# Keeping the low part of K in both partition halves, and stacking high and low compressed probabilities on 128 partitions

## The chip, the cores and the metric

The kernel runs on one core of a Trainium2 chip. A core has a matmul engine (TensorE, PE in the rows; its loads of the stationary operand are listed apart as PEld), two engines for elementwise work (VectorE or DVE, ScalarE or ACT), a slower general one (GpSimd or POOL) and an engine that issues transfers (SyncE or SP). They run their own instruction streams and meet at semaphores. The metric is the device time of one execution in microseconds, lower is better.

## The reference, cut to what matters

The program is a stack of transformer pieces on 512 tokens of width 1024, in 32-bit floats: a gated feed-forward block, a mixer with two kinds of attention, attention to a memory of 256 tokens, a second feed-forward block, sliding-window attention, and a pooling layer. The change touches the scores of three attentions with heads of 64 channels, and one small product:

```python
# forgetting attention ("fox"), 8 heads, causal
sc = einsum('bhqd,bkhd->bhqk', q, k) + c_q - c_k;  p = masked_softmax(sc);  o = p @ v
# "nsa", 8 heads in 2 groups: compressed keys, selected blocks, window
s_c = einsum('bsgjd,bcgd->bgjsc', qg, kc) + bias_c;  p_c = masked_softmax(s_c)
o_c = einsum('bgjsc,bcgd->bsgjd', p_c, vc)
o_s = softmax(qg @ k_s + bias) @ v_s          # all 8 blocks are selected: causal over 512
o_w = softmax(qg @ k_w + bias) @ v_w          # window of 512: causal over 512
o = g0 * o_c + g1 * o_s + g2 * o_w
# sliding-window attention with sinks ("swa"), 16 heads, 4 of K and V, window 128
s = q @ k / 8;  p = softmax over 2 blocks of 128 and the sink;  o = p @ v
```

## The kernel before, in words

Every matmul is made precise by splitting. A 32-bit value x is kept as a high part h (x rounded by a copy to the matmul's own 32-bit format, on ScalarE) and a low part x − h (a subtraction, on VectorE); lines 77 to 91 have the helpers `copy`, `low` and `split`. A projection of the width 1024 is eight steps of three matmuls each (lines 116 to 118: high·high, high·low, low·high) of 128 rows by 512 columns, with weights that arrive by a transfer of 512 KB and are split on arrival.

An attention with heads of 64 channels handles two heads per tile of 128 partitions. `stacked` (line 92) makes for each of the two heads e a tile q whose one half of the partitions holds the high part and the other half the low part of the same head. `doubled` (line 98) makes for K a tile per head with the high part in both halves, so that one matmul over 128 rows yields q_high·k_high + q_low·k_high. The low part of K is one tile `kl` for both heads, head e in half e. The second matmul of a score, lines 403 and 1159, uses only these 64 rows of `q` and of `kl`, and adds q_high·k_low in the same bank.

A `causal_unit` (fox and nsa, line 387) is one head: four score steps with 128, 256, 384 and 512 columns, each of two matmuls (lines 402 and 403; in fox a third one, line 405, adds the causal mask), followed on VectorE by the bias and the maximum (line 407), on ScalarE by the exponential (line 411), on VectorE by the reciprocal of the sum (line 415), and on GpSimd by the scaling of the probabilities (line 420). Four "turns" transpose the probabilities on TensorE (line 430) and split them, four "products" multiply by V (lines 442 and 443). An `swa_unit` (line 1139) has two score steps of four matmuls each (line 1158 and line 1159 alternate), the scaling on line 1179, two turns (line 1193) and two products (line 1209).

`run` (line 173) writes TensorE's order: a slot is one score step, a turn that was due some slots later, a product one or two slots after its turn, and between them projection steps from a backlog, spread evenly. TensorE keeps to that order; the other engines' order is laid out by a scheduler. In nsa each head also starts from the compressed product: lines 884 and 885 multiply the same `vcb` (high and low of compressed V, on 64 partitions) by the high and then the low compressed probabilities (`pch`, `pcl`, 64 partitions each). Fox has 4 pairs of heads, one unit a head; nsa 4 pairs, with two units a head; swa 8 pairs.

Of the kernel before, what the change touches and what calls it, by code (L numbers as in the profile page):

```python
# [38 lines left out]
def tile_net(ctx: ExitStack, tc: tile.TileContext, A: dict, out: bass.AP):  # L39
# [9 lines left out]
    def nm(s):  # L49
        uid[0] += 1  # L50
        return f"{s}_{uid[0]}"
# [46 lines left out]
    def doubled(pair, lo, t):  # L98
        for e in range(2):
            rows, other = slice(64 * e, 64 * e + 64), slice(64 - 64 * e, 128 - 64 * e)  # L100
            copy(pair[e][rows, :], t[rows, :])
            copy(pair[e][other, :], t[rows, :])
            low(lo[rows, :], t[rows, :], pair[e][rows, :])

# [281 lines left out]

    def causal_unit(pp, qk, e, bias, diag, coef, v, first, last, open_acc, close_acc, needs=()):
        rows = slice(64 * e, 64 * e + 64)
        st = {}

        def score(i):
            def go():
                if i == 0:
                    st["p"] = pp.tile([P, 1280], F32, tag="P", bufs=2, name=nm("P"))
                    st["nmx"] = small(4, "nmx")
                    st["sm"] = small(4, "sm")
                q, kd, kl = qk()
                pr, nmx, sm = st["p"], st["nmx"], st["sm"]
                n = P * (i + 1)
                b = scb()  # L400
                c = slice(P * i, P * (i + 1))
                nc.tensor.matmul(b[:, :n], q[:, c], kd[:, :n], start=True, stop=False)  # L402
                nc.tensor.matmul(b[:, :n], q[rows, c], kl[rows, :n], start=False, stop=not diag)  # L403
                if diag:
                    nc.tensor.matmul(b[:, P * i : n], ident_bf, cmask_bf, start=False, stop=True)
                sc = pp.tile([P, S], F32, tag="S", bufs=2, name=nm("S"))
                nc.vector.tensor_tensor_reduce(
                    out=sc[:, :n], in0=b[:, :n], in1=bias(i), op0=OP.add, op1=OP.min,
                    scale=-1.0, scalar=3e38, accum_out=nmx[:, i : i + 1])
                w = pr[:, OFF[i] : OFF[i] + n]  # L410
                nc.scalar.activation(w, sc[:, :n], AF.Exp, scale=-1.0,
                                     bias=nmx[:, i : i + 1], accum_out=sm[:, i : i + 1])
                if i % 2:
                    g = slice(i - 1, i + 1)
                    nc.vector.reciprocal(sm[:, g], sm[:, g])
                    if coef is not None:
                        nc.vector.tensor_mul(sm[:, g], sm[:, g], coef[:, g])
                    for z in (i - 1, i):
                        w = pr[:, OFF[z] : OFF[z] + P * (z + 1)]
                        nc.gpsimd.tensor_scalar(w, w, sm[:, z : z + 1], 1.0, op0=OP.mult,  # L420
                                                op1=OP.mult)
            return go
# [100 lines left out]
    def compress_steps(mp, sb, which, kch, kcl, vcb, tails):  # L523
# [28 lines left out]
        def tail():  # L552
# [10 lines left out]
            else:  # L563
# [3 lines left out]
                for g in range(2):  # L567
                    rw = slice(32 * g, 32 * g + 32)
                    split(vcb[rw, g, 0, :], vcb[rw, g, 1, :], b2[rw, :64])

        hw = mp.tile([P, S], F32, tag=("on0", "yf5")[which], name=nm("hw"))
# [3 lines left out]
    def mixer(acc, rep, next_tile, aside):  # L575
        with area("mix") as mp:
# [10 lines left out]
            nc.vector.memset(kcl.bitcast(F32), 0.0)  # L587
            vcb = mp.tile([64, 2, 2, HD], F32R, name="vcb")
            nc.vector.memset(vcb.bitcast(F32), 0.0)
# [46 lines left out]
            with area("fox") as fp:  # L636
# [51 lines left out]
                with area("foxq") as xp, area("att") as ap:  # L688
                    units = []
                    for p in range(4):  # L690
                        qk = {}

                        def fox_steps(p, z, qk):
                            names = ("d0", "d1", "kl") if z else ("q0", "q1")
                            for a in names:
# [9 lines left out]
                            if z:  # L705
                                return project_steps(4 + p, None, doubled, pair, qk["kl"])
                            return project_steps(p, 0.125, stacked, pair)
# [24 lines left out]
            with area("nsa") as np_, area("att") as ap:  # L732
                on += [mp.tile([P, S], F32, tag=f"on{k}", name=nm("on")) for k in range(4)]
                yf += [mp.tile([P, S], F32, tag=f"yf{k}", name=nm("yf")) for k in range(5, KD)]
                vsw = np_.tile([P, NQ, 4, 2, HD], F32R, name="vsw")
                ks = [[np_.tile([P, S], F32R, name=nm("ks")) for _ in range(3)]
                      for _ in range(2)]
# [10 lines left out]
                for p in range(4):  # L748
# [8 lines left out]
                    if p == 0:  # L757
                        each(query_steps(0, st))
                        for br in range(2):
                            each(project_steps(10 + br, None, doubled, ks[br][:2], ks[br][2]))  # L760
                        each(token_major_steps(A["mvsw"], rcol, NQ, xh, xl, store_v(vsw, (0, 4))))
                        needs = ()
                    else:
                        while log.left() < 36 * p - 20:
                            log.add(*side.pop(0))
                        needs = (log.add(query_steps(p, st), KD),)
# [28 lines left out]
    def fox_units(p, xp, ap, qk, vf, ofh, ofl, needs):  # L795
        res = {}
        units = []
        for e in range(2):
            h = 2 * p + e

            def close(acc_b, e=e):
# [6 lines left out]
            units.append(causal_unit(  # L808
                ap, lambda e=e: (qk[f"q{e}"], qk[f"d{e}"], qk["kl"]), e,
                lambda i, e=e: qk["cb", e][:, : P * (i + 1)], True, None,  # L810
# [20 lines left out]
    def nsa_units(np_, ap, p, st, ks, vsw, kch, kcl, vcb, gates, valid, o, needs):  # L831
# [34 lines left out]
        def turn():  # L866
            pc = st["pc"]
            bt = trb()
            for i in range(NQ):
                nc.tensor.transpose(bt[0:64, P * i : P * (i + 1)],  # L870
                                    pc[:, 2 * i : 2 * i + 2, :].rearrange("p e c -> p (e c)"),
                                    ident)
            pch = np_.tile([64, S], F32R, tag="pch", bufs=1, name=nm("pch"))
            pcl = np_.tile([64, S], F32R, tag="pcl", bufs=1, name=nm("pcl"))
            split(pch, pcl, bt[0:64, :])
            st["ph"] = pch, pcl

        units = [Unit([score(0), score(1)], [turn], [None], needs, 2)]
        for e in range(2):
            h = 4 * e + p  # L880

            def lead(acc_b, e=e):
                vc = pair_cols(vcb[:, e])
                nc.tensor.matmul(acc_b, vc, st["ph"][0], start=True, stop=False)
                nc.tensor.matmul(acc_b, vc, st["ph"][1], start=False, stop=False)

            acc = Accumulator(lead)
            for br in range(2):
                units.append(causal_unit(
                    ap, lambda br=br, e=e: (st["q"][e], ks[br][e], ks[br][2]), e,  # L890
                    lambda i, e=e: st["tb"][e][:, 384 - P * i :], False,
# [144 lines left out]
    def attn2(acc1, accg, next_tile):  # L1036
        with area("swa") as mp:
# [27 lines left out]
            for t2 in range(2):  # L1065
                kt = [mp.tile([P, S], F32R, name=nm("kt")) for _ in range(3)]
                t = tmp()
                nc.vector.tensor_mul(t, bk[t2], r)
                doubled(kt[:2], kt[2], t)
                ks.append(kt)  # L1070
# [31 lines left out]
            for m in range(KD):  # L1102
# [11 lines left out]
                for e in range(2):  # L1114
# [3 lines left out]
                    def close(acc_b, e=e, m=m, st=st):  # L1118
# [3 lines left out]
                        if e == 1:  # L1122
                            st["o"] = st["t"]
                            combine(m, st)

                    units.append(swa_unit(mp, st, ks[t2][e], ks[t2][2], e, band, nsk[:, hq : hq + 1],
                                          lambda j, kv=kv: pair_cols(vt[:, j, kv]), close,
# [11 lines left out]
    def swa_unit(mp, qs, kd, kl, e, band, nsk, v, close, needs):  # L1139
        rows = slice(64 * e, 64 * e + 64)  # L1140
        st = {}

        def score(i2):
            def go():
# [7 lines left out]
                for z in range(2):  # L1152
# [5 lines left out]
                    nc.tensor.matmul(b[:, d], q[:, c], kd[:, ks], start=True, stop=False)  # L1158
                    nc.tensor.matmul(b[:, d], q[rows, c], kl[rows, ks], start=False, stop=True)  # L1159
                for z in range(2):  # L1160
# [373 lines left out]
```

## Time and profile before

| what | value |
|---|---|
| median of 3 runs | 1761.22 us (1760.43 to 1761.32) |
| span of the profiled execution, first to last instruction | 1759.5 us |
| TensorE busy | 1737.4 us, 99% of the span, 8308 matmuls |
| weight loads (PEld) | 1396.9 us, 79% |
| VectorE, ScalarE, GpSimd | 966.9 us (55%), 753.6 us (43%), 231.7 us (13%) |
| DMA | 184.19 MB, mean 105 GB/s |

The span is that of one profiled execution; the median is taken from runs of their own, 1.7 us longer. TensorE's busy time counts matmuls that overlap in its pipeline, so the start of one lies before the end of the one ahead, and a mean duration is not the rate at which matmuls follow one another. That rate is read from the chain of waits, whose pieces run from one matmul's end to the next one's end, or from the starts in the timeline. Bracketed figures in a timeline row are the idle time before the instruction and what ended it.

### The profile page before, as it was taken

What the parts mean: (1) busy time and instruction counts of PE and PEld (TensorE: products, weight loads), DVE (VectorE), ACT (ScalarE), POOL (GpSimd) and SP (SyncE); (2) the same over time, 40 slices, a digit from 0 to 9 for tenths busy, and PEclk for the clock granted to TensorE, in tenths of its full rate; (3) what the DMA queues carried; (4) which work ended last, traced back from release to release, by engine and by line L of the source; (5) the groups of instructions that cost most, each with busy time, mean ns of one, the idle gap of its engine ahead of it and who ended that gap; (6) DMA issues with size and microseconds to landing.
All of it is one profiled execution on the core that took longest, in us unless ns stands there. A gap on an engine that the chain in (4) does not pass through costs nothing.

```text
span 1759.5 us, 22066 instructions
## 1 busy us (share of the span) xinstructions
PE 1737.4 (99%) x8308; PEld 1396.9 (79%) x8308; DVE 966.9 (55%) x1718; ACT 753.6 (43%) x1350; POOL 231.7 (13%) x315
## 2 busy tenths in 40 slices
PE   8999999999999999999999999999999999999997
PEld 6888878888778777777988888888888877788887
DVE  7333433336685566667655444433333677876674
ACT  6222222235675555545444432222233566644242
POOL 2000000003221222203001200000011034421001
PEclk9999999999999999999999999999999999999999
DMA  5222244433243122036531522222344321133232
GB/s 191 96 96 96 95 142 118 127 115 108 79 144 106 37 67 78 29 93 205 172 108 48 192 96 89 92 96 96 93 134 123 110 70 51 49 132 124 92 121 78
DMA packets 66255, 184.19 MB, mean 105 GB/s; under 512 B 7979, under 2 KB 13883, under 8 KB 66148
## 3 DMA queue, kind: packets, MB, share of 16 engines
q1 hardware_dynamic: 59300, 171.25, 30.0%
q10 hardware_dynamic: 6848, 11.54, 1.8%
q8 instruction: 65, 1.06, 0.2%
q14 instruction: 42, 0.34, 0.1%
HBM read 170.14 MB, written 15.24 MB: 105 GB/s over the span
## 4 chain that ended last, share of the span: by engine, by line
PE 96%; DVE 2%; ACT 1%; DMA 1%; issue 0%; SPq 0%; POOL 0%; DVEq 0%; ACTq 0%
PE mm L116 21%; PE mm L117 20%; PE mm L118 20%; PE tr L118 6%; PE tr L116 6%; PE tr L117 6%; PE tr L430 2%; PE sc L403 2%; PE pv L320 1%; PE pv L321 1%; PE pv L322 1%; PE sc L1159 1%; PE tr L1193 1%; PE pv L443 1%; PE pv L442 1%; PE sc L402 1%
## 5 line engine op out<-in xcount | busy, mean ns | idle before, releaser
L78 ACT ACTIVATE wh<-wr 128x1024 fp32r<-128x1024 f32 (+2 forms) x292 | 294.7, 1010 | 672.8 <-PE mm L117 348.3
L81 DVE TENSOR_TENSOR wl<-wr,wh 128x1024 fp32r<-128x1024 f32 (+2 forms) x291 | 342.0, 1176 | 174.6 <-ACT wh L78 170.4
L116 PE MATMUL mm<-xh,wh 128*128 128x512 f32 x872 | 359.2, 412 | 5.9 <-ACT wh L78 5.8
L117 PE MATMUL mm<-xl,wh 128*128 128x512 f32 x872 | 347.4, 398 | 0.2
L118 PE MATMUL mm<-xh,wl 128*128 128x512 f32 x872 | 346.6, 397 | 0.0
L222 POOL TENSOR_TENSOR acc<-acc,t 128x512 f32<-128x512 f32 (+1 forms) x55 | 74.8, 1367 | 959.0 <-ACT t L221 958.8
L116 PEld LDWEIGHTS mm<-xh,wh 128*128 128x128 f32 x872 | 165.9, 190 | 39.2 <-ACT wh L78 6.4
L118 PEld LDWEIGHTS mm<-xh,wl 128*128 128x128 f32 x872 | 164.9, 189 | 39.6 <-DVE wl L81 0.2
L117 PEld LDWEIGHTS mm<-xl,wh 128*128 128x128 f32 x872 | 165.5, 190 | 32.9 <-DVE xl L89 2.7
L118 PE MATMUL tr<-xh,wl 128*128 128x512 f32 x424 | 168.2, 397 | 0.5 <-DVE wl L81 0.5
L116 PE MATMUL tr<-xh,wh 128*128 128x512 f32 x424 | 168.1, 396 | 0.0
L117 PE MATMUL tr<-xl,wh 128*128 128x512 f32 x424 | 168.1, 396 | 0.0
L116 PE MATMUL mm<-hh,wh 128*128 128x512 f32 x352 | 138.9, 395 | 0.0
L117 PE MATMUL mm<-hl,wh 128*128 128x512 f32 x352 | 138.9, 395 | 0.0
L118 PE MATMUL mm<-hh,wl 128*128 128x512 f32 x352 | 138.9, 395 | 0.0
L355 DVE TENSOR_TENSOR t<-t,tr 128x512 f32<-128x512 f32 x44 | 30.3, 688 | 143.9 <-PE tr L118 142.5
L78 ACT ACTIVATE ph<-tr 128x512 fp32r<-128x512 f32 (+3 forms) x136 | 63.8, 470 | 102.6 <-PE tr L430 72.6
L118 PEld LDWEIGHTS tr<-xh,wl 128*128 128x128 f32 x424 | 79.9, 188 | 20.4 <-DVE wl L81 0.9
L117 PEld LDWEIGHTS tr<-xl,wh 128*128 128x128 f32 x424 | 79.9, 188 | 19.5
L116 PEld LDWEIGHTS tr<-xh,wh 128*128 128x128 f32 x424 | 79.8, 188 | 19.3
L81 DVE TENSOR_TENSOR pl<-tr,ph 128x512 fp32r<-128x512 f32 (+3 forms) x136 | 72.1, 531 | 37.0 <-ACT ph L78 35.5
L352 DVE TENSOR_TENSOR t<-mm,rstd 128x512 f32<-128x512 f32 x44 | 30.4, 691 | 112.1 <-PE mm L118 112.1
(344 smaller groups left out, 2994.4 us busy)
## 6 DMA issues: line engine op xcount, KB each, us to landing
wr<-in_f2gu_dram SPq DMA_DIRECT2D x44, 512.0 KB, 3.2
wr<-in_f1gu_dram SPq DMA_DIRECT2D x42, 512.0 KB, 3.2
wr<-in_mfm_dram SPq DMA_DIRECT2D x32, 512.0 KB, 3.2
xd<-xs ACTq DMA_DIRECT2D x40, 256.0 KB, 2.0
wr<-in_ain_dram SPq DMA_DIRECT2D x18, 512.0 KB, 3.3
wr<-in_f1d_dram SPq DMA_DIRECT2D x16, 512.0 KB, 3.6
xs<-xd SPq DMA_DIRECT2D x32, 256.0 KB, 3.3
wr<-in_f2d_dram SPq DMA_DIRECT2D x16, 512.0 KB, 3.6
```

The source lines that it names most:

```text
L78: nc.scalar.activation(o, i, AF.Copy, scale=scale)
L81: (eng or nc.vector).tensor_sub(o, i, h.bitcast(F32))
L116: nc.tensor.matmul(o, sh, mh, start=start, stop=False)
L117: nc.tensor.matmul(o, sh, ml, start=False, stop=False)
L118: nc.tensor.matmul(o, sl, mh, start=False, stop=stop)
L222: (nc.vector if last else nc.gpsimd).tensor_add(acc, acc, q[:, :n])
L320: mm(b, sh[k][:, tk], hi[:, c], start=first, stop=False, skip_group_check=True)
L321: mm(b, sh[k][:, tk], lo[:, c], start=False, stop=False, skip_group_check=True)
L352: nc.vector.tensor_mul(a, pg, r)
L355: nc.vector.tensor_mul(h, a, pu)
L403: nc.tensor.matmul(b[:, :n], q[rows, c], kl[rows, :n], start=False, stop=not diag)
L430: nc.tensor.transpose(b[:, P * (i - j) : P * (i - j + 1)], pr[:, OFF[i] + P * j : OFF[i] + P * (j + 1)], ident)
```

## The change

`doubled` gets two tiles for the low part, one per head, and writes each head's low part into both halves: one more subtraction on VectorE for e = 0, and one on GpSimd for e = 1. The second matmul of each score then takes all 128 rows of `q` and of the head's own tile (this also adds q_low·k_low). In nsa the compressed V is copied into the upper half of a `vcb` of 128 partitions, the high and low compressed probabilities go into the two halves of one tile `pch`, and one matmul of 128 rows takes the place of two of 64.

```diff
     def doubled(pair, lo, t):
...
-            low(lo[rows, :], t[rows, :], pair[e][rows, :])
+            low(lo[e][rows, :], t[rows, :], pair[e][rows, :])
+            low(lo[e][other, :], t[rows, :], pair[e][rows, :], nc.gpsimd if e else None)
...
-                nc.tensor.matmul(b[:, :n], q[rows, c], kl[rows, :n], start=False, stop=not diag)
+                nc.tensor.matmul(b[:, :n], q[:, c], kl[:, :n], start=False, stop=not diag)
...
                 for g in range(2):
                     rw = slice(32 * g, 32 * g + 32)
+                    up = slice(64 + 32 * g, 64 + 32 * g + 32)
                     split(vcb[rw, g, 0, :], vcb[rw, g, 1, :], b2[rw, :64])
+                    copy(vcb[up, g, :, :], vcb[rw, g, :, :].bitcast(F32))
...
-            vcb = mp.tile([64, 2, 2, HD], F32R, name="vcb")
+            vcb = mp.tile([P, 2, 2, HD], F32R, name="vcb")
...
-                            names = ("d0", "d1", "kl") if z else ("q0", "q1")
+                            names = ("d0", "d1", "kl0", "kl1") if z else ("q0", "q1")
...
-            pch = np_.tile([64, S], F32R, tag="pch", bufs=1, name=nm("pch"))
-            pcl = np_.tile([64, S], F32R, tag="pcl", bufs=1, name=nm("pcl"))
-            split(pch, pcl, bt[0:64, :])
-            st["ph"] = pch, pcl
+            pch = np_.tile([P, S], F32R, tag="pch", bufs=1, name=nm("pch"))
+            split(pch[0:64, :], pch[64:128, :], bt[0:64, :])
+            st["ph"] = pch
...
                 vc = pair_cols(vcb[:, e])
-                nc.tensor.matmul(acc_b, vc, st["ph"][0], start=True, stop=False)
-                nc.tensor.matmul(acc_b, vc, st["ph"][1], start=False, stop=False)
+                nc.tensor.matmul(acc_b, vc, st["ph"], start=True, stop=False)
...
-                    nc.tensor.matmul(b[:, d], q[rows, c], kl[rows, ks], start=False, stop=True)
+                    nc.tensor.matmul(b[:, d], q[:, c], kl[:, ks], start=False, stop=True)
```

The lists of K tiles in nsa and swa grow from three tiles to four in the same way.

TensorE's order, at the first compressed product of nsa (line 884 becomes line 886, and 116 to 118 become 117 to 119):

```order
L118 MATMUL mm_4791<-xh_71,wl_4794 128x512
L884 MATMUL pv_4801<-pch_4689,vcb 128x512
L885 MATMUL pv_4801<-pcl_4690,vcb 128x512
L442 MATMUL pv_4801<-ph_4729,vsw 128x512
L443 MATMUL pv_4801<-pl_4730,vsw 128x512
L116 MATMUL mm_4791<-xh_72,wh_4793 128x512
```

```order
L119 MATMUL mm_4810<-xh_71,wl_4813 128x512
L886 MATMUL pv_4820<-pch_4709,vcb 128x512
L442 MATMUL pv_4820<-ph_4748,vsw 128x512
L443 MATMUL pv_4820<-pl_4749,vsw 128x512
L117 MATMUL mm_4810<-xh_72,wh_4812 128x512
```

The eight matmuls of line 885 go; nothing else on TensorE changes its place, and the score matmuls stand as before.

VectorE's order where fox makes its first K (`t` is the projected K, `d` the doubled high part, `kl` the low part, line 407 the first score's bias and maximum), before and after:

```order
L603 TENSOR_TENSOR t_3079<-mm_3048,rstd_2574 128x512
L81 TENSOR_TENSOR wl_3228<-wr_3226,wh_3227 128x1024
L81 TENSOR_TENSOR kl_3047<-t_3079,d_476_3045 64x512
L81 TENSOR_TENSOR kl_3047<-t_3079,d_477_3046 64x512
L407 ISA S_3122,nmx_3116<-sc_3118,cb_3004 128x128
```

```order
L605 TENSOR_TENSOR t_3080<-mm_3049,rstd_2574 128x512
L81 TENSOR_TENSOR wl_3234<-wr_3232,wh_3233 128x1024
L81 TENSOR_TENSOR kl_478_3047<-t_3080,d_476_3045 64x512 x2
L81 TENSOR_TENSOR kl_479_3048<-t_3080,d_477_3046 64x512
L407 ISA S_3125,nmx_3119<-sc_3121,cb_3004 128x128
```

Three subtractions stand where two stood, ahead of the first score's bias and maximum.

GpSimd's order at the second pair of fox, where it scales probabilities `P` and makes one low part of `q`, before and after:

```order
L420 TENSOR_SCALAR P_3115<-P_3115,sm_3117 128x384
L420 TENSOR_SCALAR P_3115<-P_3115,sm_3117 128x512
L420 TENSOR_SCALAR P_3209<-P_3209,sm_3211 128x128
L420 TENSOR_SCALAR P_3209<-P_3209,sm_3211 128x256
L81 TENSOR_TENSOR q_518_3220<-t_3293,q_518_3220 64x512
```

```order
L420 TENSOR_SCALAR P_3118<-P_3118,sm_3120 128x384
L420 TENSOR_SCALAR P_3118<-P_3118,sm_3120 128x512
L81 TENSOR_TENSOR kl_504_3156<-t_3205,d_502_3154 64x512
L420 TENSOR_SCALAR P_3215<-P_3215,sm_3217 128x128
L420 TENSOR_SCALAR P_3215<-P_3215,sm_3217 128x256
L81 TENSOR_TENSOR q_520_3226<-t_3299,q_520_3226 64x512
```

One subtraction for the pair's second head is put in between two heads' scalings. There are eight such in the program: four in fox, two in nsa and two in swa, the last four ahead of the first scores of their stages.

## Rows read from the trace of the kernel before

**Rows 1.** The page: busy time of the engines, and the chain that ended last, by engine.
```profile
PE 1737.4 (99%) x8308; PEld 1396.9 (79%) x8308; DVE 966.9 (55%) x1718; ACT 753.6 (43%) x1350; POOL 231.7 (13%) x315
...
PE 96%; DVE 2%; ACT 1%; DMA 1%; issue 0%; SPq 0%; POOL 0%; DVEq 0%; ACTq 0%
```

**Rows 2.** TensorE's waits over the whole span, the longest one: who waited for whom, us in total, times, longest.
```profile
PE mm L116 <- ACT wh L78: 5.8, 1, 5.8
```

**Rows 3.** Instructions by source line: the 64-row matmuls of nsa, fox, swa and of the compressed product, with their number, the shortest, median and longest duration in ns, first and last start in us, and the forms.
```profile
L403 PE MATMUL sc<-ks,q x64: 322/410/503, 581.2 to 752.6; 64*128 64x128 f32 x16, 64*128 64x256 f32 x16, 64*128 64x384 f32 x16, 64*128 64x512 f32 x16
...
L403 PE MATMUL sc<-kl,q x32: 323/408/502, 438.6 to 532.9; 64*128 64x128 f32 x8, 64*128 64x256 f32 x8, 64*128 64x384 f32 x8, 64*128 64x512 f32 x8
...
L1159 PE MATMUL sc<-kt,q x64: 322/380/385, 1407.9 to 1541.2; 64*128 64x256 f32 x48, 64*128 64x128 f32 x16
...
L884 PE MATMUL pv<-pch,vcb x8: 492/501/502, 596.9 to 754.1; 64*128 64x512 f32 x8
```

**Rows 4.** Timeline of the weight loads around the first score step of nsa: start us, us, instruction, idle before it.
```profile
580.84 0.19 PEld L402 LDWEIGHTS sc<-ks,q 128*128 128x128 f32 x1
581.22 0.18 PEld L403 LDWEIGHTS sc<-ks,q 64*128 64x128 f32 x1 [0.19 <-issue]
581.47 0.19 PEld L116 LDWEIGHTS mm<-xh,wh 128*128 128x128 f32 x1
```

**Rows 5.** Chain of waits in nsa, a score step of 256 columns with a projection behind it: start us, us from the end of the piece before to its own end, what.
```profile
582.43 0.11 PE sc L402
582.54 0.31 PE sc L403
582.85 0.43 PE mm L116
583.28 0.24 PE mm L117
```

**Rows 6.** The same view in fox: products, that is pairs of matmuls that both use 128 rows, of 256 and of 128 columns, the latter with a projection behind.
```profile
475.99 0.12 PE pv L442
476.10 0.12 PE pv L443
...
479.34 0.06 PE pv L442
479.40 0.11 PE pv L443
479.51 0.28 PE mm L116
```

**Rows 7.** The same view: four transposes behind a 64-row score matmul in nsa; four behind a projection's matmul of 128 rows; the mask matmul and four transposes in fox behind a 64-row score matmul.
```profile
601.02 0.59 PE tr L430 x4
...
537.91 0.44 PE tr L430 x4
...
478.04 0.16 PE sc L405
478.20 0.44 PE tr L430 x4
```

**Rows 8.** The same view in swa: the second score step of a head, four matmuls of 256 columns, and the projection behind it.
```profile
1411.18 0.12 PE sc L1158
1411.29 0.31 PE sc L1159
1411.60 0.31 PE sc L1158
1411.92 0.31 PE sc L1159
1412.22 0.43 PE mm L116
```

**Rows 9.** The same view in nsa: the compressed product and the first product of 512 columns.
```profile
596.97 0.43 PE pv L884
597.40 0.23 PE pv L885
597.63 0.43 PE pv L442
598.05 0.23 PE pv L443
```

**Rows 10.** Busy time of the engines in the stages of fox, nsa and swa: stretch and its length in us, then TensorE, weight loads, VectorE, ScalarE, GpSimd (instructions), granted clock as a share of full speed, DMA share and GB/s.
```profile
438.00:552.00 114.00, 112.63 (x584) 85.49 (x583) 81.04 (x180) 74.14 (x159) 22.31 (x37) 1.00 0.32 107
577.00:766.00 189.00, 188.94 (x893) 136.76 (x892) 120.12 (x352) 102.86 (x252) 42.53 (x85) 1.00 0.17 51
1407.00:1557.00 150.00, 150.00 (x739) 116.19 (x738) 119.88 (x329) 98.44 (x258) 55.80 (x79) 1.00 0.17 57
```

**Rows 11.** The subtractions that make low parts: on VectorE for K in fox, on GpSimd for q (shortest, median, longest in ns).
```profile
L81 DVE TENSOR_TENSOR kl<-t,d x8: 674/686/1047, 437.1 to 489.9; 64x512 fp32r<-64x512 f32 x8
...
L81 POOL TENSOR_TENSOR q<-t,q x16: 1272/1370/1815, 431.8 to 1526.5; 64x512 fp32r<-64x512 f32 x16
```

**Rows 12.** Places where another engine is just in time: a piece of the chain of waits in fox; and in nsa the timeline of GpSimd's last two scalings of a head and of the four transposes that read them.
```profile
489.94 1.05 DVE kl L81
...
590.29 1.25 POOL L420 TENSOR_SCALAR P<-P,sm 128x384 f32<-128x384 f32 x2 [4.86 <-DVE sm L417]
...
591.47 0.66 PE L430 MATMUL tr<-ident,P 128*128 128x128 f32 x4
```

More of the change, by code (lines that the diff above doesn't have):

```diff
@@ L385, in ffn, with causal_unit @@
             return residual(body, next_tile)
-    def causal_unit(pp, qk, e, bias, diag, coef, v, first, last, open_acc, close_acc, needs=()):
-        rows = slice(64 * e, 64 * e + 64)
+    def causal_unit(pp, qk, bias, diag, coef, v, first, last, open_acc, close_acc, needs=()):
         st = {}
@@ L705, in fox_steps @@
                             if z:
-                                return project_steps(4 + p, None, doubled, pair, qk["kl"])
+                                return project_steps(4 + p, None, doubled, pair,
+                                                     [qk["kl0"], qk["kl1"]])
                             return project_steps(p, 0.125, stacked, pair)
@@ L735, in mixer @@
                 vsw = np_.tile([P, NQ, 4, 2, HD], F32R, name="vsw")
-                ks = [[np_.tile([P, S], F32R, name=nm("ks")) for _ in range(3)]
+                ks = [[np_.tile([P, S], F32R, name=nm("ks")) for _ in range(4)]
                       for _ in range(2)]
@@ L759, in mixer @@
                         for br in range(2):
-                            each(project_steps(10 + br, None, doubled, ks[br][:2], ks[br][2]))
+                            each(project_steps(10 + br, None, doubled, ks[br][:2], ks[br][2:]))
                         each(token_major_steps(A["mvsw"], rcol, NQ, xh, xl, store_v(vsw, (0, 4))))
@@ L808, in fox_units @@
             units.append(causal_unit(
-                ap, lambda e=e: (qk[f"q{e}"], qk[f"d{e}"], qk["kl"]), e,
+                ap, lambda e=e: (qk[f"q{e}"], qk[f"d{e}"], qk[f"kl{e}"]),
                 lambda i, e=e: qk["cb", e][:, : P * (i + 1)], True, None,
@@ L889, in nsa_units @@
                 units.append(causal_unit(
-                    ap, lambda br=br, e=e: (st["q"][e], ks[br][e], ks[br][2]), e,
+                    ap, lambda br=br, e=e: (st["q"][e], ks[br][e], ks[br][2 + e]),
                     lambda i, e=e: st["tb"][e][:, 384 - P * i :], False,
@@ L1065, in attn2 @@
             for t2 in range(2):
-                kt = [mp.tile([P, S], F32R, name=nm("kt")) for _ in range(3)]
+                kt = [mp.tile([P, S], F32R, name=nm("kt")) for _ in range(4)]
                 t = tmp()
                 nc.vector.tensor_mul(t, bk[t2], r)
-                doubled(kt[:2], kt[2], t)
+                doubled(kt[:2], kt[2:], t)
                 ks.append(kt)
@@ L1124, in close @@
                             combine(m, st)
-                    units.append(swa_unit(mp, st, ks[t2][e], ks[t2][2], e, band, nsk[:, hq : hq + 1],
+                    units.append(swa_unit(mp, st, ks[t2][e], ks[t2][2 + e], e, band, nsk[:, hq : hq + 1],
                                           lambda j, kv=kv: pair_cols(vt[:, j, kv]), close,
@@ L1139, in swa_unit @@
     def swa_unit(mp, qs, kd, kl, e, band, nsk, v, close, needs):
-        rows = slice(64 * e, 64 * e + 64)
         st = {}
```

## The prediction

> **What bounds the kernel now.** I read the page first: TensorE is busy for 99% of the span and makes 96% of the chain that ended last, VectorE and ScalarE stand at 55% and 43% [rows 1]. The table of waits by engine says the same from the other side: the longest wait of TensorE in the whole span is one of 5.8 us [rows 2]. The windows over the three stages that the change touches show TensorE busy for 112.6 of 114 us in fox, 188.9 of 189 in nsa and all of 150 in swa, at a granted clock of 1.00, which is the level of 2.4 GHz [rows 10]. So the rate at which matmuls follow one another is the time, and a nanosecond off that rate counts until another engine is late.
>
> That rate stands in the pieces of the chain of waits, not in the durations of the rows by line (a 64-row score matmul "lasts" 410 ns [rows 3], but its neighbours run under it). In nsa the first matmul of a score step with 256 columns and 128 rows adds 0.11 us, the second one with 64 rows adds 0.31, and the projection's matmul behind it 0.43, where the next one of the same form adds 0.24 [rows 5]. A product in fox is two matmuls that both use 128 rows: with 256 columns they add 0.12 and 0.12 [rows 6]. So a 64-row matmul costs 0.31 − 0.12 = 0.19 us more than one of 128 rows with as many columns, and the 128-row matmul behind it 0.43 − 0.24 = 0.19 more. The weight loads show how: the 64-row one begins only after an idle 0.19 us at its own matmul's place, and the load of line 116 again only at the end of that [rows 4]. It is a price of going from 128 rows to 64 and back: line 885, 64 rows behind 64 rows, adds 0.23 like a projection, while 884 ahead of it and 442 behind it add 0.43 each [rows 9].
>
> **The change part by part.** The 160 score matmuls of 64 rows (64 + 32 + 64 [rows 3]) become matmuls of 128 rows in the same places; the diff of the order shows nothing else moved on TensorE but the eight of line 885, which go.
>
> In nsa 64 steps lose their two changes. Most have a turn behind them, since the slot puts it there: four transposes add 0.59 behind 64 rows and 0.44 behind 128 [rows 7], so the second change costs 0.15 there, and a step saves 0.19 + 0.15 = 0.34 (0.38 with a projection behind). 64 × 0.34 = 21.8 us. With 128 columns a pair of 128-row matmuls is too short for its own weight loads: the second adds 0.11 and not 0.06, the projection behind 0.28 and not 0.24 [rows 6]. So these steps save 0.09 less; 16 of them make 1.4. Nsa: 20.3 us.
>
> In fox the mask's matmul stands behind the 64-row one and adds 0.16; the transposes behind it add their plain 0.44 [rows 7]. How the mask matmul follows one of 128 rows no row shows. It can't fall much below 0.06, what 128 columns add elsewhere [rows 6], so the second change is worth 0 to 0.10. I take 0.05, the middle: 32 × 0.24 = 7.7, less 8 × 0.09 = 0.7, makes 7.0 us (5.4 to 8.6).
>
> In swa a step is four matmuls, with four changes: 0.12 + 0.31 + 0.31 + 0.31 and 0.43 behind, 1.48 us [rows 8]; with 128 rows it is 4 × 0.12 + 0.24 = 0.72. That saves 0.76, or 0.72 with transposes behind. 32 × 0.72 = 23.0, less 16 × 0.09 = 1.4 for the 128-column ones: 21.6 us.
>
> The compressed product: 0.43 + 0.23 + 0.43 become two plain matmuls, 1.32 with the last 0.23 against 3 × 0.23 = 0.69 [rows 9]; 8 × 0.63 = 5.0 us.
>
> Off TensorE: 20.3 + 7.0 + 21.6 + 5.0 = 53.9 us.
>
> What is added: eight subtractions on VectorE, by the row of the same form 0.69 us each, and eight on GpSimd, by the row for q 1.37 us [rows 11]. The pairs of nsa and swa lie under the V projection that follows them in the code (32 steps of three matmuls with 256 columns, 0.12 each by [rows 6], 11.5 us), so they cost nothing. The first K of fox stands bare ahead of the first score: 0.7 us. The two copies of compressed V on ScalarE lie at the end of fox behind a backlog of projections: nothing. The upper half of `pch` is the same subtraction with another target half: nothing, as the low part of q is written across halves in the same time [rows 11].
>
> What is late next: other engines that were just in time. In fox the low part of K is a piece of the chain already, 1.05 us [rows 12]; three later pairs each get one subtraction of 0.69 more ahead of them, of which I count half, 1.0 us. A head's turns begin two slots behind its last score. With three score steps in between faster by some 0.34, 0.25 and 0.25, they come 0.85 us sooner. At the head shown, GpSimd ends its scaling at 591.54 and the transposes that read it began at 591.47 [rows 12], so nothing is spare and this head loses most of the 0.85. Others have more room; between no head and all 24 (20 us) I take one in six as an estimate: 24 × 0.85 / 6 = 3.4 us. In swa VectorE has 119.9 us to do [rows 10], and TensorE needs 150 − 21.6 = 128.4: 93%, so I count 1 us. Together 0.7 + 1.0 + 3.4 + 1.0 = 6.1.
>
> Net 53.9 − 6.1 = 47.8 us: the span goes from 1759.5 to 1711.7. The runs' median lies 1.7 us above that span, and I carry this over: 1761.2 − 47.8 = 1713.4 us.
>
> **The rivals.** First, VectorE becomes the bound in swa. For: no stage in the rows shows it above 0.80 of the time (119.9 of 150) with TensorE not stopped, and after the change it would be 0.93, in an order that is fixed. Against: TensorE didn't stop once at 0.80 [rows 10]. If 0.80 is the ceiling, swa keeps its 150 us and the time is 1713.4 + 20.6 = 1734; if half is lost, 1724. In fox (81.0 + 2.8 of 107) and nsa (120.1 of 164) it stays at or below 0.79.
>
> Second, the rows are not what costs: the second matmul of a score shares q with the first, or its load can't be hidden for another reason, and with 128 rows it still adds 0.31. Then only the eight matmuls of line 885 go, 8 × 0.23 = 1.8 us: 1759.4. Against it: products also use one stationary operand twice, and add 0.12 [rows 6].
> The Trainium skill, TensorE: Matmul & The Clock Gate, Part 3, says that a weight load overlaps with matmuls in flight only where the row groups differ. By that rule 128 rows behind 128 rows would be the worst case, and this rival would come out. The trace disagrees: products of 256 columns add 0.12 [rows 6], less than the 0.19 that one load takes [rows 4].
>
> Third, slower: TensorE stops so often for VectorE and GpSimd in swa and fox that the granted clock falls to the level of 1.2 GHz, where its work takes twice as long. From 54 us of such work on, the whole gain is eaten; at half of the 235 us that both stages would have left it is 118 us more, 1761.2 − 53.9 + 118 = 1825. Against it: the stops of 1.4 us in fox left the clock at 1.00 [rows 10].
>
> **How the numbers follow.** The forecast gets 0.74, VectorE as the bound 0.20, no gain from rows 0.03, the clock 0.03. The forecast's own range: 1704, if nothing is late, the mask's change is worth all of its 0.10, and the rounding of the pieces (0.01 × 160) falls well; 1722, if late engines eat two and a half times what I count. For 8 in 10 I reach to most of the second case: 1703 to 1732. Faster by over 0.2% (3.5 us, about what a measurement of this kernel can tell) are the first two cases, 0.94; the third is within 0.2%, 0.03; slower 0.03.
>
> **What would show it.** In the chain of waits of the changed kernel the second matmul of a score of 256 columns adds 0.12 and the projection behind it 0.24; four matmuls of an swa step 0.12 each; its weight loads have no idle time of 0.19 ahead. Fox should take some 110 us, nsa 168, swa 130. If swa stays above 140 with VectorE over 0.85 busy, the first rival holds; if the second score matmul still adds 0.3, the second; a granted clock under 1.00, the third. Waits of TensorE on GpSimd's scaling of over 5 us in sum would make my 3.4 too small.

## The result and the profile after

The changed kernel takes 1717.99 us (median of 4 runs, 1717.27 to 1720.67) against 1761.09 us for the kernel before (4 runs, 1760.43 to 1761.32). The ratio is 0.9758, with a 95% interval of 0.9744 to 0.9772. The forecast was 1713.4 us: 43 us went where 48 were expected.

The page of the changed kernel, its first lines and the chain by engine, answers to [rows 1]:

```profile
span 1716.3 us, 22080 instructions
...
PE 1683.8 (98%) x8300; PEld 1390.8 (81%) x8300; DVE 976.4 (57%) x1726; ACT 753.8 (44%) x1352; POOL 246.2 (14%) x323
...
PE 88%; DVE 6%; ACT 2%; POOL 1%; issue 1%; DMA 0%; SPq 0%; DVEq 0%; ACTq 0%; POOLq 0%
```

TensorE is busy for 53.6 us less (1737.4 − 1683.8). The part of the span in which it is not busy grew from 22.1 to 32.5 us. The second number is the news of this page: TensorE's share of the chain fell from 96% to 88%, so other engines now set the pace in places. TensorE's waits over the whole span name those places. Columns as in [rows 2]; the first row is the one that stood there before.

```profile
PE mm L117 <- ACT wh L78: 6.0, 1, 6.0
PE sc L1158 <- DVE q L81: 3.4, 4, 1.2
PE tr L430 <- POOL P L420: 1.5, 4, 0.6
PE mm L530 <- DVE u L537: 1.4, 1, 1.4
...
PE pv L443 <- DVE pl L81: 0.9, 1, 0.9
...
PE tr L1193 <- DVE sm L1175: 0.7, 1, 0.7
```

Next come the places that the prediction named, in the chain of waits: a score step of nsa with a projection behind it, which answers to [rows 5]; a step of 128 columns in fox with its mask; a first step of swa; and the compressed product, which answers to [rows 9].

```profile
578.19 0.12 PE sc L402
578.31 0.12 PE sc L403
578.43 0.24 PE mm L117
...
442.13 0.12 PE sc L402
442.25 0.12 PE sc L403
442.36 0.07 PE sc L405
...
1421.68 0.06 PE sc L1158
1421.74 0.11 PE sc L1159
1421.86 0.17 PE sc L1158
1422.03 0.12 PE sc L1159
1422.14 0.33 PE tr L1193 x3
...
590.95 0.23 PE pv L886
591.18 0.23 PE pv L442
591.41 0.23 PE pv L443
```

The second score matmul adds 0.12 us where it added 0.31, and the projection behind it 0.24 where it added 0.43. The second matmul pair of the swa step adds 0.17 + 0.12, where one 64-row matmul alone added 0.31. The compressed product and the first matmul behind it add a plain 0.23 each. The weight loads show why, in the timeline of a score step that answers to [rows 4]:

```profile
581.18 0.19 PEld L402 LDWEIGHTS sc<-ks,q 128*128 128x128 f32 x1
581.42 0.19 PEld L403 LDWEIGHTS sc<-ks,q 128*128 128x128 f32 x1
```

No idle time stands in brackets: the load for the second score matmul starts 0.24 us after the first one's, without the idle 0.19 us that it had before.

The stages in the windows view, columns as in [rows 10]:

```profile
439.00:548.00 109.00, 104.90 (x584) 85.27 (x583) 87.22 (x184) 74.94 (x161) 29.14 (x41) 1.00 0.34 112
577.00:738.00 161.00, 160.12 (x865) 133.97 (x864) 114.63 (x346) 99.84 (x247) 42.28 (x84) 1.00 0.19 59
1379.00:1511.00 132.00, 127.09 (x725) 108.90 (x725) 115.75 (x329) 98.14 (x257) 56.00 (x78) 1.00 0.20 65
```

The granted clock is 1.00 in all three, the level of 2.4 GHz. But TensorE now stands still for 4.1 us of fox (1.4 before), 0.9 of nsa (0.1 before), and 4.9 of swa (none before). To compare lengths I take marks that both traces have, the start of a stage's first score matmul and the end of its last product:

| stretch | before, us | after, us | difference |
|---|---|---|---|
| start to the first fox score | 438.46 | 439.46 | +1.00 |
| first fox score to first nsa score | 142.61 | 137.66 | −4.95 |
| nsa, first score to last product | 183.94 | 160.37 | −23.57 |
| nsa's end to first swa score | 642.77 | 642.31 | −0.46 |
| swa, first score to last product | 146.66 | 130.94 | −15.72 |
| rest | 205.07 | 205.52 | +0.45 |

The rows sum to −43.25, which is the difference of the spans. The first fox score starts between 438.2 and 439.5 in the traces of all kernels in this study, whether its subtractions were added or not. In the first 20 us of the trace, ahead of anything that the change touches, TensorE's stops sum to 6.3 us before and 8.1 us after, and from there to the first fox score neither trace has one of over 0.15 us; so the 1 us isn't made by the subtractions. The row of −0.46 holds two things that are no part of the savings: a new stop of 0.69 us ahead of the first swa score, and the clock. Behind two stops of 1.22 and 0.90 us that both traces have, the granted clock of the kernel before was 0.50 from 835 to 837 us, the level of 1.2 GHz, while the changed kernel kept 1.00. So some 1.2 us (0.46 + 0.69) of the 43.25 are the luck of these two executions.

### The profile page after: what moved, and what is told of

It reads as the page before. It is cut to its first block, busy times and chain, and to the rows that moved or that the text cites. A ratio compares the mean times of both kernels' runs of the same rounds, so it can differ in the third digit from the quotient of the medians.

```text
span 1716.3 us, 22080 instructions
## 1 busy us (share of the span) xinstructions
PE 1683.8 (98%) x8300; PEld 1390.8 (81%) x8300; DVE 976.4 (57%) x1726; ACT 753.8 (44%) x1352; POOL 246.2 (14%) x323
## 4 chain that ended last, share of the span: by engine, by line
PE 88%; DVE 6%; ACT 2%; POOL 1%; issue 1%; DMA 0%; SPq 0%; DVEq 0%; ACTq 0%; POOLq 0%
PE mm L117 20%; PE mm L118 20%; PE mm L119 20%; PE tr L119 6%; PE tr L118 6%; PE tr L117 6%; PE tr L430 1%; PE pv L321 1%; DVE wl L81 1%; PE pv L322 1%; PE pv L323 1%; PE pv L443 1%; PE sc L403 1%; DVE pl L81 1%; PE pv L442 1%
```

## The experiments

All kernels of this section compute the whole reference. Medians and ratios are against runs of the kernel before on the same chip.

**The price: is it the 64 rows or the change of rows?** In the kernel before, I put the two 128-row matmuls of an swa step first and the two 64-row ones behind them. The work is the same; two changes of rows per step go.

```diff
-                for z in range(2):
-                    ...
-                    nc.tensor.matmul(b[:, d], q[:, c], kd[:, ks], start=True, stop=False)
-                    nc.tensor.matmul(b[:, d], q[rows, c], kl[rows, ks], start=False, stop=True)
+                for rw, k2 in ((slice(0, P), kd), (rows, kl)):
+                    for z in range(2):
+                        ...
+                        nc.tensor.matmul(b[:, d], q[rw, c], k2[rw, ks], start=k2 is kd and z == 0,
+                                         stop=k2 is kl and z == 1, skip_group_check=True)
```

> The kernel before, with the four score matmuls of an swa step put in another order: both of 128 rows, then both of 64 rows. The number of 64-row matmuls stays, the changes between 128 and 64 rows fall from four to two a step. Theory (a change of rows costs 0.19 us each): a step falls from 1.48 to 0.12 + 0.12 + 0.31 + 0.12 + 0.43 = 1.10 us in the chain, 32 x 0.38 = 12 us, so 1749 us, up to 1752 if VectorE starts to stop TensorE. Rival (a 64-row matmul costs 0.38 us more by itself, wherever it stands): 1761 us, and the second 64-row matmul still adds 0.31.

Measured: 1750.72 us (1750.47 to 1751.04) against 1761.21, ratio 0.994 (0.9925 to 0.9955). The chain of waits at the step of [rows 8], with the four matmuls on one row:

```profile
1411.15 0.66 PE sc L1159 x4
1411.80 0.43 PE mm L116
```

The four add 0.66 us where they added 0.12 + 0.31 + 0.31 + 0.31 = 1.05. That is 2 × 0.12 + 0.31 + 0.12: a 64-row matmul behind another on the same rows costs no more than a 128-row one. The timeline agrees: by their ends the second 64-row matmul adds 0.11 us, and its weight load runs from 1411.41 to 1411.60, under the matmul ahead. The price is of the change from 128 rows to 64 and back, not of 64 rows, and the projection still pays the way back with its 0.43. The Trainium skill, TensorEngine Tiling (Array Packing), Key Properties, says that changing the tiling mode, not just the tile, drains TensorE. The trace agrees that a change has a price, 0.19 us each; that it is a drain no run here shows. The rule weighed in the prediction (the Trainium skill, TensorE: Matmul & The Clock Gate, Part 3), by which loads overlap only where row groups differ, doesn't hold here: the second 64-row matmul uses the same rows as the first, and its load is hidden all the same. The swa stretch fell from 146.66 to 135.86 us, by 10.8 where 12 were expected, and TensorE has no stop in it.

**The compressed product alone.** The kernel before with only `vcb` on 128 partitions and the stacked `pch`.

```diff
-                nc.tensor.matmul(acc_b, vc, st["ph"][0], start=True, stop=False)
-                nc.tensor.matmul(acc_b, vc, st["ph"][1], start=False, stop=False)
+                nc.tensor.matmul(acc_b, vc, st["ph"], start=True, stop=False)
```

> The kernel before with the stacked compressed product alone. Theory: 8 x 0.63 = 5.0 us less, 1756.1 us, nothing else is late. Rival (the heads whose scaling is just in time eat it): 1759 us or more.

Measured: 1755.34 us (1753.68 to 1756.51) against 1761.21, ratio 0.9966 (0.9953 to 0.9979). The nsa stretch shrank by 4.9 us, from 183.94 to 179.0, against 5.0 in the prediction. The medians differ by 5.9; the trace shows why they can differ by more than the stretch, since its clock stays at 1.00 where that of the kernel before fell to 0.50 (835 to 837 us).

**The added work alone.** The changed kernel with every score's second matmul back on 64 rows. The eight subtractions on each engine and the stacked product stay. (The added subtractions without the stacked product weren't run.)

```diff
-                nc.tensor.matmul(b[:, :n], q[:, c], kl[:, :n], start=False, stop=not diag)
+                nc.tensor.matmul(b[:, :n], q[rows, c], kl[rows, :n], start=False, stop=not diag)
...
-                    nc.tensor.matmul(b[:, d], q[:, c], kl[:, ks], start=False, stop=True)
+                    nc.tensor.matmul(b[:, d], q[rows, c], kl[rows, ks], start=False, stop=True)
```

> The changed kernel with its score matmuls back on 64 rows: the K tiles, the 16 added subtractions and the stacked product stay. Theory (the subtractions cost 0.7 us at the first K of fox and little else; the 5 us short of the 54 lie in new stops of TensorE that come with its speed): 1761.1 - 5.0 + 0.7 to 1.7, so 1757 to 1758 us. Rival (the subtractions themselves cost what is missing): 1761 us or more.

Measured: 1757.57 us (1756.38 to 1758.93) against 1761.21, ratio 0.9979 (0.997 to 0.9988). Compared with the product alone, the fox stretch is 143.69 us against 142.65: the subtractions cost 1.0 us there. Nsa takes the same in both. The medians differ by 1.2 us more. That is the clock again, as far as the record tells: all five runs of the product alone had a mean granted clock of 0.998, of this kernel's ten only five had, and the median of those five is 1756.46 us, 1.1 above the 1755.34 of the product alone.

**Swa alone undone.** The changed kernel with only swa's scores back on 64 rows (the second part of the diff above).

> The changed kernel with swa's score matmuls back on 64 rows (its added subtractions stay). Theory by the two traces: swa's stage, first score to last product, fell from 146.7 to 130.9 us, so 15.7 us come back: 1733.7 us. Rival (swa was worth its whole 21.6 us of TensorE time and the missing part was lost in fox and nsa): 1738 us or more.

Measured: 1735.02 us (1733.59 to 1735.57) against 1761.21, ratio 0.9849 (0.9832 to 0.9865). The swa stretch went back to 146.76 us, and TensorE's stops in it are gone; a stop of 0.37 us ahead of its first score stays. So swa's share of the gain is 17.0 us by the medians and 15.8 by the stretch, and the stretch is the better measure: in this trace fox took 139.27 us where the changed kernel took 137.66, with nearly the same stops (4.2 and 4.1), because the granted clock fell to 0.55 from 471 to 473 and 0.59 from 473 to 475, right behind two of them. The subtractions that were added ahead of swa stay in this kernel and cost nothing inside the stretch while TensorE is slower.

**What stops TensorE in swa.** The longest stop within the stage, in the trace of the changed kernel: VectorE's timeline, then TensorE's.

```profile
1450.53 0.67 DVE L1081 SCALAR_TENSOR_TENSOR t<-mm,rstd 128x512 f32<-128x512 f32 x1
1451.12 1.21 DVE L81 TENSOR_TENSOR wl<-wr,wh 128x1024 fp32r<-128x1024 f32 x1
1452.36 0.68 DVE L81 TENSOR_TENSOR q<-t,q 64x512 fp32r<-64x512 f32 x1
```

```profile
1453.10 0.33 PE L1158 MATMUL sc<-kt,q 128*128 128x128 f32 x1 [1.24 <-DVE q L81]
```

A score waits for the low part of its q, and on VectorE that subtraction stands behind the split of a weight (1.21 us) which no score needs. Two readings are open: VectorE has too much to do in this stage (the prediction's first rival), or single instructions come late in an order that leaves them no room. Two edits tell them apart: one projects q one slot earlier and leaves VectorE's work as it is, the other takes 32 instructions off VectorE.

```diff
-        run(units, log, tail=4, look=1, hold=2)
+        run(units, log, tail=4, look=2, hold=2)
```

> The changed kernel with swa's queries projected one slot earlier (look=2), no work added or removed. Theory (in swa the first score of a pair stops for the low part of q, which VectorE makes behind a weight split; 3.4 us in four stops): these stops go, 1718.0 - 3.4 = 1714.6 us, with the stops for the scalings (1.3 us) left. Rival (VectorE's work in swa is the bound as such, at 0.88 of the time): the stops move elsewhere, 1717 to 1718 us.

Measured: 1713.85 us (1712.18 to 1714.81) against 1761.34, ratio 0.9731 (0.9717 to 0.9744). The swa stretch is 127.12 us, 3.8 less than in the changed kernel. Its window and the waits of TensorE that lie in the stage:

```profile
1380.00:1509.00 129.00, 126.61 (x729) 109.55 (x728) 113.32 (x331) 98.97 (x259) 55.88 (x78) 1.00 0.20 66
```

```profile
PE tr L1193 <- POOL pr L1179: 1.7, 2, 1.2
...
PE sc L1158 <- DVE q L81: 0.7, 1, 0.7
```

The only wait for a low part of q that is left is the one ahead of the stage's first score; those inside the stage are gone, while VectorE's share stayed at 0.88 (113.32 of 129, 115.75 of 132 in the changed kernel). Without its remaining 1.7 us of stops the stretch would be 21.2 us below the kernel before, by the prediction's sum 21.6.

The other edit:

```diff
-                nc.vector.tensor_scalar(es, nmx[:, g], nsk, None, op0=OP.subtract)
-                nc.scalar.activation(es, es, AF.Exp)
+                nc.scalar.activation(es, nmx[:, g], AF.Exp, bias=sk)
```

> The changed kernel with the sink's difference in swa taken into ScalarE's exponential (a bias instead of VectorE's subtraction of line 1172): 32 instructions of 0.31 us less on VectorE, 9.9 us of its 118.5 in swa, and none more on ScalarE. Theory (the stops are at single late subtractions): VectorE reaches them a little earlier, half of the 4.2 us of idle in swa go: 1716 us. Rival (VectorE's work is the bound): nearly all go, 1713.5 us.

Measured: 1715.67 us (1715.50 to 1716.23) against 1761.34, ratio 0.9742 (0.9729 to 0.9756). The swa stretch is 128.57 us, 2.4 less than in the changed kernel. Of the 4.2 us of stops 2.5 are left, 1.66 of them in one stop for q's low part: nearly half went, as the theory said. Both edits together:

> Both edits to swa at once. Theory (swa's missing part is the 4.2 us of stops): swa's stage falls from 130.9 to 126.5 us and the time to 1713.5 us. Rival (the transposes and score matmuls of 128 columns cost more than the sum said): stops go, but the stage stays above 128 us, 1715 us.

Measured: 1715.09 us (1714.02 to 1717.54) against 1761.34, ratio 0.9741 (0.9727 to 0.9754). This missed: 1713.5 was expected, and it is no faster than the first edit alone, though VectorE has less to do (967.7 us in the span against 972.6). The time is that of the rival and the stretch of 129.18 us is above its 128, but not by its reason, since stops of 2.2 us are left in the stretch. They come from another late instruction, GpSimd's scaling of probabilities, and the longest one has a consequence. The waits, TensorE's timeline, and the windows view from 1496 to 1498 us (columns as in [rows 10]):

```profile
PE tr L1195 <- POOL pr L1181: 2.2, 2, 1.9
```

```profile
1493.91 0.33 PE L1195 MATMUL tr<-ident,pr 128*128 128x128 f32 x1 [1.85 <-POOL pr L1181]
```

```profile
1496.00:1498.00 2.00, 2.00 (x6) 1.54 (x5) 1.23 (x6) 1.12 (x6) 1.16 (x3) 0.50 0.00 0
```

Behind the stop of 1.85 us the granted clock fell to 0.50, the level of 1.2 GHz, and a projection's matmul adds 0.43 us there where it adds 0.23 to 0.24 otherwise. The stretch is 2.06 us longer than with the first edit alone; 0.5 of that are longer stops, the other 1.5 the clock. So this run doesn't show that the two edits work against each other.

The stops are single instructions that are late by the order, and each new order has others. Less work on VectorE helped (2.4 us of the stretch), a change of order alone took back more (3.8), so the amount of VectorE's work is not the bound.

**More room in fox.** Products in fox held back one slot more.

```diff
-        run(units, log, hold=1)
+        run(units, log, hold=2)
```

> The changed kernel with fox's products one slot later (hold=2), no work added or removed. Theory (at the third pair of fox the products stop for the split of the transposed probabilities, which stands behind four copies and three subtractions for K; 0.64 + 0.94 us): this stop goes, 1716.4 us, the other three of fox (2.5 us) stay. Rival (the stretch is bound by ScalarE and VectorE, so the stop moves to the next score): 1717.5 to 1718 us.

Measured: 1718.81 us (1716.74 to 1721.16) against 1761.34, ratio 0.976 (0.9747 to 0.9774). The runs spread over both forecasts; the stretch decides for the rival: fox took 138.10 us, not less than 137.66. The stops at products are gone and others have come, for VectorE's work, though at projections and a transpose and not at the next score as the rival had it (the changed kernel had 1.4 in the first of these rows, and neither of the others):

```profile
PE mm L530 <- DVE u L537: 1.7, 1, 1.7
...
PE tr L430 <- DVE kcl L81: 1.2, 1, 1.2
PE mm L117 <- DVE yf L613: 1.2, 2, 0.7
```

**What a subtraction costs beside GpSimd.** The stop at the third pair of fox in the changed kernel: VectorE, GpSimd and TensorE in the timeline.

```profile
468.32 3.11 DVE L81 TENSOR_TENSOR kl<-t,d 64x512 fp32r<-64x512 f32 x3
471.47 0.56 DVE L81 TENSOR_TENSOR pl<-tr,ph 128x384 fp32r<-128x384 f32 x1
...
468.89 1.29 POOL L81 TENSOR_TENSOR kl<-t,d 64x512 fp32r<-64x512 f32 x1 [2.80 <-ACT d L78]
...
472.08 0.45 PE L443 MATMUL pv<-pl,vf 128*128 128x384 f32 x1 [0.94 <-DVE pl L81]
```

Three subtractions of 0.69 us took 3.11 while GpSimd made the fourth. By the rows by line the longest of the three took 1.70. To see whether GpSimd's work is what stretches them, I took the version with q a slot earlier in swa and put the eight subtractions of GpSimd on VectorE.

```diff
-            low(lo[e][other, :], t[rows, :], pair[e][rows, :], nc.gpsimd if e else None)
+            low(lo[e][other, :], t[rows, :], pair[e][rows, :])
```

> The kernel with swa's queries a slot earlier (look=2), and with the eight subtractions that the change put on GpSimd done by VectorE instead. Theory (the two engines slow each other: at the third pair of fox one of VectorE's subtractions took 1.70 us and not 0.69 while GpSimd made its own): VectorE's four take 4 x 0.69 = 2.8 us there against 3.1 for three, none over 1.1 us, the products behind them come no later, and the stretch from fox's first score to nsa's first stays at 137.7 us or below. Rival (the 1.70 us had another cause, and a fourth subtraction of 0.69 us per pair comes on top): the stretch grows by about 2 us, to 139.7.

Measured: 1712.55 us (1711.89 to 1713.44) against 1760.04, ratio 0.9727 (0.9711 to 0.9743). The fox stretch is 138.01 us, 0.3 above what the theory allowed and 1.7 below the rival. Fox as a whole gained nothing: at the third pair the stops fell from 1.58 to 1.23 us, but the fourth pair has a new one of 0.69. At the third pair VectorE makes all four in less time than three before:

```profile
467.29 2.78 DVE L81 TENSOR_TENSOR kl<-t,d 64x512 fp32r<-64x512 f32 x4
470.10 0.56 DVE L81 TENSOR_TENSOR pl<-tr,ph 128x384 fp32r<-128x384 f32 x1
```

At the start of swa it is plainer. Rows by source line for the low parts of swa's first K (number, then shortest, median and longest duration in ns), in the version that differs only in this edit (on VectorE and on GpSimd), and then in this one:

```profile
L81 DVE TENSOR_TENSOR kt<-t,kt x6: 670/1188/1827, 1372.7 to 1378.2; 64x512 fp32r<-64x512 f32 x6
...
L81 POOL TENSOR_TENSOR kt<-t,kt x2: 1398/1469/1540, 1373.7 to 1376.2; 64x512 fp32r<-64x512 f32 x2
```

```profile
L81 DVE TENSOR_TENSOR kt<-t,kt x8: 675/686/691, 1372.3 to 1377.2; 64x512 fp32r<-64x512 f32 x8
```

Beside GpSimd a subtraction takes 1.69 to 1.83 us (three of the six), alone 0.69. The 1.83 us are beside GpSimd's subtraction for q, which the kernel before has too; the other two are beside the added ones. The first swa score in the timeline of TensorE, in the same two:

```profile
1380.99 0.33 PE L1158 MATMUL sc<-kt,q 128*128 128x128 f32 x1 [0.68 <-DVE q L81]
```

```profile
1379.79 0.32 PE L1158 MATMUL sc<-kt,q 128*128 128x128 f32 x1
```

The stop of 0.68 us ahead of it (0.69 in the changed kernel) is gone. This version and the one with q a slot earlier are the fastest that ran; their intervals overlap, so which of the two is faster stays open.

## Why the prediction was right, and where it was off

**What bounds the kernel, and the mechanism.** Right. The 0.19 us are paid for each change of rows; the first experiment shows it apart from everything else, and the chain after shows each piece as forecast.

**Savings on TensorE** (stretches with the stops taken out). Predicted 53.9 us; the busy time fell by 53.6. Nsa with the product: 23.6 + 0.9 − 0.1 = 24.4 against 25.3, the product's 4.9 against 5.0 in a run of its own. Fox: 4.95 + 4.1 − 1.4 = 7.7 against 7.0. The step "I take 0.05, the middle" for the mask was too low: its matmul adds 0.07 where it added 0.16, so the change was worth 0.09, within the bounds given (the sum would be 8.2). Swa: 21.2 against 21.6, read in the version that has few stops. In the trace of the changed kernel the same sum gives 19.9, because a stop costs more than its idle time: the matmul behind it adds its whole 0.33 us (the row at 1453.10) where a short one adds 0.06 to 0.12. Without their stops the stretches are 125.4 us in the two versions with two stops, 126.1 in the one with four, and 126.7 in the two with seven, so by an estimate from these about 0.26 us a stop, and 124.9 with none: a saving of 21.8 us.

**What is late next.** Here the forecast went wrong in size.
- "In swa VectorE has 119.9 us to do … so I count 1 us" is the mis-sized term. The stretch shrank by 15.7 and not 21.2 us, so lost time is some 5.5 us. Stops make 4.2 of that (the window's 4.9 less the 0.69 ahead of the first score). The step from a mean load of 93% to a loss of 1 us failed: the loss comes from single instructions, above all q's low part behind a weight's split. The trace before shows the room between that subtraction and the score that reads it: 5 to 10 us for the second to fifth pair, and 1.96, 1.78 and 1.92 us for the last three, which are those that stop inside the stage after the change. The sixth pair in that trace:

```profile
1488.62 0.69 DVE L81 TENSOR_TENSOR q<-t,q 64x512 fp32r<-64x512 f32 x1
```

```profile
1491.27 0.22 PE L1158 MATMUL sc<-kt,q 128*128 128x128 f32 x1
```

A pair has four score steps, each shorter by 0.72 us in the prediction's sum, so the next pair's first score comes up to 2.9 us sooner; if VectorE's work comes no sooner, that is 1 us more than the room of 1.9 (an estimate from these rows). Measured were 1.24, 0.49 and 1.00.
- "The pairs of nsa and swa lie under the V projection … so they cost nothing" held for nsa, where no stop stands ahead of the first score. In swa it failed by 0.69 us: three of the six subtractions took 1.68 to 1.83 us beside GpSimd's, not 0.69.
- "The first K of fox stands bare": no stop stands ahead of the first fox score in the trace after, so the 0.7 us did not show.
- Fox's later pairs: 1.0 us predicted, 1.0 measured by the experiment that has only the added work. The place is mainly the third pair. The stretching there is the lesser part of it: with all four subtractions on VectorE, none stretched, the stops at that pair were only 0.35 us shorter.
- Heads that are just in time, "one in six as an estimate": 3.4 us was too much for nsa, where the stops sum to 0.9; the head shown in [rows 12] lost 0.34 us, not most of 0.85. (The 168 us named for nsa are of a window 5 us longer than the stretch; like for like they are 163, against 160.4.) Waits for GpSimd's scaling sum to 1.5 us in the span, not over 5. Fox has the rest, 2.7 us of new stops less the 1.0 just named.

Together the stops in the stretches grew by 2.7 + 0.8 + 4.2 = 7.7 us where 6.1 were counted. The miss of 4.6 us in the span (43.2 against 47.8) is this 1.6 us, savings smaller by 1.9 if the stretch of swa is read with the stops of its own trace (15.7 + 4.2 = 19.9), and 1.0 us outside the stages. Part of the nearness is luck: 0.7 us for the first K of fox and 0.8 for the heads (2.6 of 3.4) that did not come, 0.7 more saved in fox, and in the spans some 1.2 us of the clock, stand against the 4.5 too little that was counted in swa.

**The rivals.** The first, VectorE as the bound in swa, fell as a mechanism: swa took 130.9 us, well below 140, with VectorE at 0.88 (115.75 of 132), and at the same share of 0.88 a mere change of order took back 3.8 us. What was right in it is the place. The second fell: the second score matmul adds 0.12. The third fell in size: the changed kernel's clock stayed at 1.00 through all stops. Its mechanism exists, in small. The same two stops at fox's third pair were followed by a granted clock of 0.55 in the version with swa undone and 0.53 in the one with less work on VectorE (472 to 474 us), and fox took 139.3 and 139.2 us there instead of 137.7; with both edits to swa it came behind one stop of 1.85 us. Each fall cost some 1.5 us, not the 118 of the rival.

## What to carry to other kernels

Where TensorE is the bound, read the chain for what a matmul adds to the one ahead, and look for matmuls on 64 rows between matmuls on 128: filling the other rows, even with a copy of the operand, or putting the 64-row ones side by side takes out 0.19 us a change. When the busiest engine gets faster, don't charge the next engine by its mean load; list the instructions that it has to end just before TensorE reads them, and see what stands ahead of each on that engine and how much room it has in the trace before. A small helper that is put on GpSimd can cost VectorE more than it saves it.

## What was not expected of the hardware

A VectorE subtraction with both operands in SBUF, 64 by 512, takes 0.69 us by itself and up to 1.83 us while GpSimd makes one of the same form (1.29 to 1.54 us). The two kernels compared differ only in the engine of eight subtractions, so the stretching by GpSimd is shown. The kernel before has it already, at a low part of q, while the prediction priced the added ones at 0.69 and 1.37 us each:

```profile
443.38 1.27 POOL L81 TENSOR_TENSOR q<-t,q 64x512 fp32r<-64x512 f32 x1 [9.85 <-ACT q L78]
```

```profile
443.49 1.71 DVE L81 TENSOR_TENSOR q<-t,q 64x512 fp32r<-64x512 f32 x1
```

The Trainium skill, SBUF — State Buffer, Terms, says that VectorE and GpSimd share one pair of ports, that an instruction holds it to its end and that the other engine waits meanwhile. The traces agree: whichever of two such subtractions begins second ends a fixed time after the end of the first. VectorE's ended some 0.55 us after GpSimd's here (445.20 against 444.65), at fox's third pair in the changed kernel (470.72 against 470.18), and three times ahead of swa. Where GpSimd began second, it ended 1.15 us after VectorE, and took up to 1.81 us instead of 1.27 in the kernel before.

Two 64-row matmuls in a row on the same rows of `q` cost, beyond the first change, no more than 128-row ones: 0.12 us for 256 columns. So the way back from a row change is paid once for a group of them, and grouping gave 10.5 us of swa's gain without any copy of K.
